# Kept left sums and more seven-product pairs in the closing products of a two-layer decoder trunk

## The chip, the cores and the metric

The kernel runs on one core of a Trainium2 chip, in one launch. The metric is device microseconds of one execution, as the median of several. The engines that matter are TensorE (PE, matrix products and transposes), VectorE (DVE, elementwise work), ScalarE (ACT, casts and copies) and SyncE (SP), whose queue issues the DMA transfers of the weights. Each engine works through its own instructions in order and waits where an input or a free buffer is missing.

## The reference

Two decoder layers over 256 rows of width 2048, all in float32. Layer 0 mixes tokens by retention (8 heads), layer 1 by latent attention (MLA); each is followed by a SwiGLU feed-forward block of width 5632. Every sub-layer is wrapped in two RMS norms.

```python
for i in range(DEPTH):                      # DEPTH = 2
    h = rms_norm(x, norm_mix_pre[i])
    h = retention(h, ...) if i % 2 == 0 else mla(h, ...)
    x = x + rms_norm(h, norm_mix_post[i])
    h = rms_norm(x, norm_ffn_pre[i])
    x = x + rms_norm(swiglu(h, ffn_w_gu[i], ffn_w_down[i]), norm_ffn_post[i])

def swiglu(x, w_gu, w_down):
    gate, up = jnp.split(x @ w_gu, [D_FF], axis=-1)
    return (jax.nn.silu(gate) * up) @ w_down
```

Three products close a sub-layer: the retention's output (4096 to 2048, `rto` in the kernel), the MLA's output (2048 to 2048, `mlo`), and the down product of each feed-forward block (5632 to 2048, `dn`).

## The kernel before

**Tiling.** The 256 rows are two row tiles of 128. A product runs over k-tiles of 128 (its inner dimension) and over column groups of 1024, in four banks of 128x512: `b00` and `b01` for row tile 0, `b10` and `b11` for row tile 1. A float32 value is split into two parts, `hi` (a cast, on ACT) and `lo` (the rest, a subtraction on DVE), and each product is three matmuls: hi by hi, hi by lo and lo by hi. A k-tile costs 12 matmuls of 128x512, a pair of k-tiles 24.

**Weights.** They stream through the core once. SP loads a tile of 128x1024 (512 KB) into one of four `raw` buffers; `split` makes `hi` and `lo` in rings of five buffers each (`weights`). In gate and up (`gu`), in the retention's q/k and v/g products, `tile_load` gives the last one or two k-tiles of a group other space for hi and lo, borrowed from tiles that aren't filled yet (`spare`).

**Sevens.** A pair of k-tiles by two row tiles by two column halves is a 2x2 block product, and some pairs are made with seven products in place of eight (Winograd's form): 21 matmuls. That needs sums of four blocks of the left side (`left_sums`, four 128x128 operations and a split on DVE), sums of the weights (`right_sums`: four 128x512 operations on DVE, L250 to L253, and two splits of 128x1024), and three extra banks `m` that are combined at the end: after the last seven of a product, `combine` (L340 to L345) forms the combinations on DVE, and `add` (L350) adds one to each of the four banks. The adds of row tile 0 stand in the plan behind the first k-tile pair after the last seven, the adds of row tile 1 one pair later.

**Closing products.** `closing` runs a product in two column halves, one after the other. `parted` splits the left side of the next pair and, if that pair is a seven, makes its left sums, for each half anew. The sevens are the pairs 2, 5, 8, 11, 14, 17 of 22 in both halves of the down products, and the pairs 2, 6, 10 of 16 in both of the retention output; the MLA output has none. In the second half the last four k-tiles are skewed: row tile 0 runs ahead and row tile 1 follows, so that the norm's statistics of row tile 0 start early, and the last two k-tiles of row tile 0 go bank by bank.

**Gate and up.** Eleven groups per layer (`gu0_0` to `gu0_10`, `gu1_0` and on), each with 16 k-tiles. From the second group on, the first eight k-tiles are four sevens in a form of its own (`first_sevens`): the weights' sums are called a, b, c and d, each with hi and lo. Behind each group ACT takes the silu of the gate half, DVE multiplies it by the up half into `fa` (L995), PE transposes `fa` in two batches of four (L962, banks `ftp`) and ACT copies the result (`aT`), the left side of the down product. `later(n, ...)` puts such work n loading steps into the next group.

**Order.** The program's order on each engine is set by the kernel's plan lists and then by a scheduler. Loads are issued in the order of use; a load waits for its `raw` buffer to be free.

Of the kernel before, what the change touches and what calls it, by code (L numbers as in the profile page):

```python
# [35 lines left out]
DN_SEVENS = (2, 5, 8, 11, 14, 17)  # L36
RTO_SEVENS = (2, 6, 10)
# [20 lines left out]
def trunk(  # L58
# [141 lines left out]

    def split(hi, lo, src, g=None):

        if g is None:
            nc.scalar.copy(out=hi, in_=src)  # L204
            nc.vector.tensor_sub(out=lo, in0=src, in1=hi.bitcast(F32))  # L205
# [6 lines left out]
    def weights(load, parts, name, room=None):  # L212

        raw = wp.tile([P, 1024], F32, tag="raw", bufs=RAW, name=f"{name}_raw")
# [4 lines left out]
        else:  # L219
            hi, lo = room(f"{name}_xhi"), room(f"{name}_xlo")  # L220
# [312 lines left out]
    def tile_load(w, g, name, halves=0, spare=(0, None)):  # L533
# [4 lines left out]
        def load(kt, first_half=False):  # L538
# [8 lines left out]
            return weights(dma, parts, f"{name}_w{kt}", spare[1] if kt >= DT - spare[0] else None)  # L547
# [6 lines left out]
    hT = hp.tile([P, DT, 2, NT, P], F32R, tag="hT", name="hT")  # L554
# [21 lines left out]
    def norm_piece(t, i, ssq, col):  # L576
# [13 lines left out]
        split(hT[:, ks, 0, t, :], hT[:, ks, 1, t, :], part)  # L590
# [31 lines left out]
    def closing(act, kts, w, g_post, col, name, gain_tile, skew=4, sevens=(), sums=None):  # L622
# [36 lines left out]

        parted(0, 0)  # L660
        for half in range(2):
# [45 lines left out]
            def first_done(banks):  # L707
# [11 lines left out]
                between=first_done if half else None, sevens=sevens,  # L719
                left=lambda p, half=half: parts["s", half, p],  # L720
# [16 lines left out]
    def retention():  # L737
# [43 lines left out]
        with tc.tile_pool(name="rt_s", bufs=1) as sp:  # L781
# [81 lines left out]
            with tc.tile_pool(name="rt_v", bufs=1) as rp:  # L863
# [3 lines left out]
                def spare_y(name):  # L867
                    return rp.tile([P, 1024], F32R, tag="yT", bufs=RH, name=name)
# [61 lines left out]
                def sums():  # L930
                    both = ("vh", "vl")[sums.n % 2]
                    sums.n += 1
                    s = rp.tile([P, 2, 4, P], F32R, tag=both, bufs=1, name="rs")
# [7 lines left out]
                    lambda name: rp.tile([P, 1024], F32, tag="sg", bufs=1, name=name), sevens=RTO_SEVENS, sums=sums,  # L941
# [3 lines left out]
    def swiglu(i):  # L945
        with tc.tile_pool(name=f"ff{i}", bufs=1) as fp:
# [4 lines left out]
            def spare_a(name):  # L951
                return fp.tile([P, 1024], F32R, tag="aT", bufs=groups, name=name)
# [14 lines left out]
            def sums(n=0):  # L967
# [12 lines left out]
            for j in range(groups):  # L980
                name = f"gu{i}_{j}"
                spare = min(2, (groups - j) // 2), spare_a
# [8 lines left out]
                for t in range(NT):  # L991
# [385 lines left out]
```

## Time and profile before

| what | value |
|---|---|
| time, median of 3 runs | 2427.02 us (2423.98 to 2428.43) |
| the profiled execution, its own time | 2426.71 us |
| its span, first to last instruction | 2424.9 us |
| mean granted TensorE clock | 0.998 |
| ACT busy | 1479.1 us (61%) |
| DMA | 463.75 MB, 191 GB/s |

The profile's page gives busy times of each engine; a window gives the same for a stretch of the span. A row of the timeline has the start, the duration, the engine, the line, and what is written from what; in brackets stand the idle time ahead of it and what ended that. Matmuls are pipelined: a 128x512 matmul shows some 0.39 us of duration, while the next starts earlier, so their cost is read from start to start. A row of the chain of waits has a start, a duration, an engine and line, and the number of instructions. In a row of groups stand, behind the first bar, the busy time and the mean ns of one, and behind the second the idle time ahead of the group and its releaser. The stages follow each other so (us from the start of the span): the retention up to about 560, its output to 733, gate and up of layer 0 to 1207, its down product to 1440 (first half up to 1324), MLA with its output up to about 1710, gate and up of layer 1 to 2184, its down product to the end.

### The profile page before, as it was taken

What the parts mean: (1) busy time and instruction counts of PE and PEld (TensorE: products, weight loads), DVE (VectorE), ACT (ScalarE), POOL (GpSimd) and SP (SyncE); (2) the same over time, 40 slices, a digit from 0 to 9 for tenths busy, and PEclk for the clock granted to TensorE, in tenths of its full rate; (3) what the DMA queues carried; (4) which work ended last, traced back from release to release, by engine and by line L of the source; (5) the groups of instructions that cost most, each with busy time, mean ns of one, the idle gap of its engine ahead of it and who ended that gap; (6) DMA issues with size and microseconds to landing.
All of it is one profiled execution on the core that took longest, in us unless ns stands there. A gap on an engine that the chain in (4) does not pass through costs nothing.

```text
span 2424.9 us, 30707 instructions
## 1 busy us (share of the span) xinstructions
PE 2403.3 (99%) x10888; PEld 1975.1 (81%) x10888; DVE 2122.0 (88%) x3034; ACT 1479.1 (61%) x2082; POOL 23.9 (1%) x38
## 2 busy tenths in 40 slices
PE   9999999999999999999999999999999999999998
PEld 7888888888888787888888888888877888888887
DVE  8878989887879999899989987876899999998997
ACT  6545666665656666666666665655666666666664
POOL 0000000000000000000000000000000000000000
PEclk9999999999999999999999999999999999999999
DMA  7565565556665565656456654446656565556655
GB/s 273 171 211 185 164 206 194 165 172 203 192 213 193 195 213 184 217 172 216 168 194 214 207 185 148 130 137 198 202 182 215 180 211 202 188 183 202 206 194 164
DMA packets 129610, 463.75 MB, mean 191 GB/s; under 512 B 14640, under 2 KB 15024, under 8 KB 129456
## 3 DMA queue, kind: packets, MB, share of 16 engines
q1 hardware_dynamic: 129456, 461.80, 57.7%
q8 instruction: 85, 1.39, 0.2%
q14 instruction: 69, 0.57, 0.1%
HBM read 459.64 MB, written 2.10 MB: 190 GB/s over the span
## 4 chain that ended last, share of the span: by engine, by line
PE 80%; DVE 12%; DMA 4%; issue 2%; ACT 2%; SPq 0%; POOL 0%; DVEq 0%; ACTq 0%; POOLq 0%
PE gu_b L409 23%; PE dn_b L409 16%; PE rvg_b L409 14%; PE rto_b L409 6%; PE rqk_b L409 5%; PE mlo_b L409 3%; PE q L409 3%; PE dn_m L409 3%; DMA gu_w_raw<-w_gu 2%; DVE gu_blo L205 2%; DVE gu_alo L205 1%; PE mc_b L409 1%; DVE gu_w_lo L205 1%; DVE gu_t L449 1%; DVE gu_clo L205 1%
## 5 line engine op out<-in xcount | busy, mean ns | idle before, releaser
L409 PE MATMUL gu_b<-gu_w_hi,hT 128*128 128x512 f32 x1248 | 342.0, 390 | 0.0
L409 PEld LDWEIGHTS gu_b<-gu_w_hi,hT 128*128 128x128 f32 x1248 | 233.1, 188 | 49.0 <-DVE hT L205 0.9
L204 ACT CAST dn_w_hi<-dn_w_raw 128x1024 fp32r<-128x1024 f32 (+1 forms) x176 | 172.8, 993 | 95.2 <-DMA dn_w_raw<-w_down 44.4
L205 DVE TENSOR_TENSOR gu_w_lo<-gu_w_raw,gu_w_hi 128x1024 fp32r<-128x1024 f32 x156 | 185.5, 1218 | 48.4 <-ACT gu_w_hi L204 48.3
L204 ACT CAST gu_w_hi<-gu_w_raw 128x1024 fp32r<-128x1024 f32 x156 | 158.1, 1048 | 92.9 <-DMA gu_w_raw<-w_gu 73.2
L205 DVE TENSOR_TENSOR dn_w_lo<-dn_w_raw,dn_w_hi 128x1024 fp32r<-128x1024 f32 (+1 forms) x176 | 196.1, 1146 | 9.2 <-ACT dn_w_hi L204 8.9
L409 PE MATMUL gu_b<-gu_w_lo,hT 128*128 128x512 f32 x624 | 193.3, 390 | 0.0
L409 PE MATMUL dn_b<-dn_w_hi,dn_ah 128*128 128x512 f32 x536 | 169.3, 390 | 0.0
L409 PE MATMUL dn_b<-dn_w_lo,dn_ah 128*128 128x512 f32 x536 | 169.0, 389 | 0.0
L409 PE MATMUL dn_b<-dn_w_hi,dn_al 128*128 128x512 f32 x536 | 168.9, 389 | 0.0
L409 PE MATMUL rvg_b<-rvg_w_hi,hT 128*128 128x512 f32 x552 | 149.8, 390 | 0.0
L409 PEld LDWEIGHTS gu_b<-gu_w_lo,hT 128*128 128x128 f32 x624 | 116.6, 188 | 25.3 <-DVE gu_w_lo L205 1.3
L409 PEld LDWEIGHTS rvg_b<-rvg_w_hi,hT 128*128 128x128 f32 x552 | 103.4, 188 | 21.4
L409 PEld LDWEIGHTS dn_b<-dn_w_hi,dn_al 128*128 128x128 f32 x536 | 100.6, 188 | 21.0
L409 PEld LDWEIGHTS dn_b<-dn_w_lo,dn_ah 128*128 128x128 f32 x536 | 100.6, 188 | 20.9
L409 PEld LDWEIGHTS dn_b<-dn_w_hi,dn_ah 128*128 128x128 f32 x536 | 100.3, 188 | 20.4
L409 PE MATMUL rqk_b<-rqk_w_hi,hT 128*128 128x512 f32 x384 | 106.0, 392 | 2.2 <-ACT rqk_w_hi L204 1.5
L204 ACT CAST gu_ahi<-gu_ta 128x1024 fp32r<-128x1024 f32 x80 | 84.3, 1054 | 35.1 <-DVE gu_ta L452 17.1
L205 DVE TENSOR_TENSOR rvg_w_lo<-rvg_w_raw,rvg_w_hi 128x1024 fp32r<-128x1024 f32 x69 | 82.3, 1222 | 25.5 <-ACT rvg_w_hi L204 25.1
L204 ACT CAST gu_bhi<-gu_t 128x512 fp32r<-128x512 f32 x80 | 49.7, 621 | 85.9 <-DVE gu_t L449 85.8
L204 ACT CAST rvg_w_hi<-rvg_w_raw 128x1024 fp32r<-128x1024 f32 x69 | 71.1, 1051 | 46.0 <-DMA rvg_w_raw<-ret_vg 34.7
L205 DVE TENSOR_TENSOR gu_alo<-gu_ta,gu_ahi 128x1024 fp32r<-128x1024 f32 x80 | 97.7, 1221 | 0.0
(487 smaller groups left out, 6109.5 us busy)
## 6 DMA issues: line engine op xcount, KB each, us to landing
gu_w_raw<-w_gu SPq DMA_DIRECT2D x192, 512.0 KB, 4.3
dn_w_raw<-w_down SPq DMA_DIRECT2D x176, 512.0 KB, 4.4
gu_s<-w_gu SPq DMA_DIRECT2D x160, 512.0 KB, 4.4
rvg_w_raw<-ret_vg SPq DMA_DIRECT2D x80, 512.0 KB, 4.4
rto_w_raw<-ret_out SPq DMA_DIRECT2D x64, 512.0 KB, 4.4
rqk_w_raw<-ret_qk SPq DMA_DIRECT2D x51, 512.0 KB, 4.5
rvg_s<-ret_vg SPq DMA_DIRECT2D x48, 512.0 KB, 4.3
mlo_w_raw<-mla_out SPq DMA_DIRECT2D x32, 512.0 KB, 3.6
```

Of the source, the lines that this page charges most:

```text
L204: nc.scalar.copy(out=hi, in_=src)
L205: nc.vector.tensor_sub(out=lo, in0=src, in1=hi.bitcast(F32))
L409: nc.tensor.matmul(out, e[2](), e[3](), start=bank not in begun, stop=ends[bank, added.get(bank, 0)] == n, skip_group_check=bank in added,)
L449: nc.vector.tensor_add(out=t2[p], in0=ta[:, 0:512], in1=b11)
```

## The change

It has four parts.

1. The left sums of a closing product are made once, when a pair first needs them, and kept for the second half. Their space is the former one tile `hT` (the normalised left side of the products before), which is now four tiles of four k-tiles each, in a ring of four with the sums; the name `hx(k)` replaces it in code.
2. The sevens differ by half: the down products have six in the first half as before and eight in the second (10 and 19 are new, 19 is the last); the retention output has four and five in place of three and three.
3. `share` divides the borrowed space in gate and up, q/k and v/g: next to hi and lo for the last one or two k-tiles, up to two raw tiles of the k-tiles ahead of the last two are put there.
4. The transposes of `fa` come two loading steps later.

```diff
-DN_SEVENS = (2, 5, 8, 11, 14, 17)
-RTO_SEVENS = (2, 6, 10)
+DN_SEVENS = (2, 5, 8, 11, 14, 17), (2, 5, 8, 10, 11, 14, 17, 19)
+RTO_SEVENS = (3, 6, 9, 12), (3, 5, 6, 9, 12)
...
+    def share(slots, room):
+
+        both = 2 if slots >= 6 else 1 if slots >= 3 else 0
+        return min(2, slots - 2 * both), both, room
...
-        raw = wp.tile([P, 1024], F32, tag="raw", bufs=RAW, name=f"{name}_raw")
+        if raw_room is None:
+            raw = wp.tile([P, 1024], F32, tag="raw", bufs=RAW, name=f"{name}_raw")
+        else:
+            raw = raw_room(F32, f"{name}_xraw")
...
-            return weights(dma, parts, f"{name}_w{kt}", spare[1] if kt >= DT - spare[0] else None)
+            raws, both, room = spare
+            return weights(
+                dma, parts, f"{name}_w{kt}", room if DT - 2 - raws <= kt < DT - 2 else None,
+                room if kt >= DT - both else None,
+            )
...
-    hT = hp.tile([P, DT, 2, NT, P], F32R, tag="hT", name="hT")
+
+    hT = {}
+
+    def hx(k):
+        if k // 4 not in hT:
+            hT[k // 4] = hp.tile([P, 4, 2, NT, P], F32R, tag="h8", bufs=4, name="hT")
+        return hT[k // 4]
...
-            if b in sevens:
-                f, hi, lo = sums()
+            if b in sevens[half] and b not in sums:
+                if len(sums) % 2 == 0:
+                    room[0] = hp.tile([P, 2, 2, 4, P], F32R, tag="h8", bufs=4, name=f"{name}_s")
+                f = wp.tile([P, 4, P], F32, tag="mv", bufs=MV, name=f"{name}_sf")
+                hi, lo = (room[0][:, len(sums) % 2, i] for i in range(2))
                 left_sums(a[:, 0, 0], a[:, 1, 0], a[:, 0, 1], a[:, 1, 1], f, hi, lo)
-                parts["s", half, b] = hi, lo
+                sums[b] = hi, lo
...
+        hT.clear()
         parted(0, 0)
...
-                between=first_done if half else None, sevens=sevens,
-                left=lambda p, half=half: parts["s", half, p],
+                between=first_done if half else None, sevens=sevens[half],
+                left=lambda p: sums[p],
...
-                        banks = vg_group(h, (min(2, (RH - h) // 2), spare_y))
+                        banks = vg_group(h, share(RH - h, spare_y))
...
-                spare = min(2, (groups - j) // 2), spare_a
+                spare = share(groups - j, spare_a)
...
-                    later(2 + t, lambda j=j, t=t, a=a: transposes(j, t, a))
+                    later(4 + t, lambda j=j, t=t, a=a: transposes(j, t, a))
```

The left out lines pass `hx(k)` where `hT` stood, give the new arguments on, and remove the two functions that made space for left sums in `rto` and `dn`. In the program the 128x512 matmuls go from 9854 to 9833. On DVE the 128x512 operations go from 1359 to 1385, the 128x128 ones from 196 to 160, the 128x1024 ones from 861 to 868. The transfers on SP are 899 before and after.

**DVE, second half of layer 0's down product, behind pair 8** (`w8_ta` and `w8_tb` are sums of pair 8's weights, that is of k-tiles 16 and 17; `w18` is a k-tile). Before:

```order
L205 TENSOR_TENSOR dn01_w8_talo_12123<-dn01_w8_ta_12116,dn01_w8_tahi_12122 128x1024
L205 TENSOR_TENSOR dn01_w8_tblo_12127<-dn01_w8_tb_12117,dn01_w8_tbhi_12126 128x1024
L205 TENSOR_TENSOR dn0_al_12152<-aT05_8859,dn0_ah_12151 128x512
L205 TENSOR_TENSOR dn01_w18_lo_12158<-dn01_w18_raw_12155,dn01_w18_hi_12157 128x1024
L205 TENSOR_TENSOR dn01_w19_lo_12176<-dn01_w19_raw_12173,dn01_w19_hi_12175 128x1024
L205 TENSOR_TENSOR dn01_w20_lo_12207<-dn01_w20_raw_12204,dn01_w20_hi_12206 128x1024
L205 TENSOR_TENSOR dn01_w21_lo_12225<-dn01_w21_raw_12222,dn01_w21_hi_12224 128x1024
```

And of the change, at the same place:

```order
L210 TENSOR_TENSOR dn01_w8_talo_12117<-dn01_w8_ta_12110,dn01_w8_tahi_12116 128x1024
L259 TENSOR_TENSOR dn01_w10_ta_12209<-dn01_w20_raw_12197 128x512
L260 TENSOR_TENSOR dn01_w10_ta_12209<-dn01_w20_raw_12197,dn01_w21_raw_12203 128x512
L210 TENSOR_TENSOR dn01_w8_tblo_12121<-dn01_w8_tb_12111,dn01_w8_tbhi_12120 128x1024
L261 TENSOR_TENSOR dn01_w10_tb_12210<-dn01_w10_ta_12209,dn01_w21_raw_12203 128x512
L210 TENSOR_TENSOR dn0_al_12146<-aT05_8920,dn0_ah_12145 128x512
L210 TENSOR_TENSOR dn01_w18_lo_12160<-dn01_w18_raw_12155,dn01_w18_hi_12157 128x1024
L210 TENSOR_TENSOR dn01_w19_lo_12178<-dn01_w19_raw_12175,dn01_w19_hi_12177 128x1024
L210 TENSOR_TENSOR dn01_w20_lo_12200<-dn01_w20_raw_12197,dn01_w20_hi_12199 128x512
L262 TENSOR_TENSOR dn01_w10_tb_12210<-dn01_w10_tb_12210,dn01_w21_raw_12203 128x512
L210 TENSOR_TENSOR dn01_w21_lo_12206<-dn01_w21_raw_12203,dn01_w21_hi_12205 128x1024
```

Two sums of pair 10 (of k-tiles 20 and 21) now stand ahead of the last split of pair 8.

**The end of the same product, DVE** (`mv` and `mx` are the combinations, `b00` to `b11` the banks). Before, where the last seven is pair 17:

```order
L205 TENSOR_TENSOR dn01_w38_lo_12629<-dn01_w38_raw_12626,dn01_w38_hi_12628 128x1024
L343 TENSOR_TENSOR dn01_mv1_12572<-dn01_m5_11846,dn01_mv1_12572 128x512
L345 TENSOR_TENSOR dn01_mx_12578<-dn01_m5_11846,dn01_mv2_12573 128x512
L205 TENSOR_TENSOR dn0_al_12623<-aT010_10719,dn0_ah_12622 128x512
L350 TENSOR_TENSOR dn01_b00_11721<-dn01_b00_11721,dn01_mv0_12571 128x512
L350 TENSOR_TENSOR dn01_b01_11722<-dn01_b01_11722,dn01_mv1_12572 128x512
```

Of the change, where it is pair 19:

```order
L210 TENSOR_TENSOR dn01_w42_lo_12697<-dn01_w42_raw_12694,dn01_w42_hi_12696 128x1024
L352 TENSOR_TENSOR dn01_mv1_12656<-dn01_m5_11858,dn01_mv1_12656 128x512
L354 TENSOR_TENSOR dn01_mx_12662<-dn01_m5_11858,dn01_mv2_12657 128x512
L210 TENSOR_TENSOR dn01_w43_lo_12703<-dn01_w43_raw_12700,dn01_w43_hi_12702 128x1024
L359 TENSOR_TENSOR dn01_b00_11742<-dn01_b00_11742,dn01_mv0_12655 128x512
L359 TENSOR_TENSOR dn01_b01_11743<-dn01_b01_11743,dn01_mv1_12656 128x512
```

A 1024-wide split of the last k-tile takes the place of a 512-wide one ahead of the adds. On PE, before, the twelve matmuls of row tile 1 for k-tiles 36 and 37 stand between the last matmul of row tile 0 that the adds wait for and the next one into `b00`; of the change, nothing does:

```order
L418 MATMUL dn01_b00_11742<-dn01_w41_lo_12683,dn0_ah_12604 128x512
L418 MATMUL dn01_b01_11743<-dn01_w41_lo_12683,dn0_ah_12604 128x512
L418 MATMUL dn01_b00_11742<-dn01_w41_hi_12682,dn0_al_12605 128x512
L418 MATMUL dn01_b01_11743<-dn01_w41_hi_12682,dn0_al_12605 128x512
L418 MATMUL dn01_b00_11742<-dn01_w42_hi_12696,dn0_ah_12664 128x512
L418 MATMUL dn01_b00_11742<-dn01_w42_lo_12697,dn0_ah_12664 128x512
```

The add into `b00` (L359 above) belongs between the third and the fifth of these rows.

**Gate and up of layer 0, group 4, PE** (`ftp030` and `ftp031` are the transposes of group 3's `fa`; `bhi`, `ahi` and so on are this group's weight sums). Before, the transposes stand behind nine matmuls of the group:

```order
L409 MATMUL gu0_4_b10_8093<-gu0_4_ahi_8103,sl0_6616 128x512
L962 MATMUL ftp030_8124<-cst_73,fa_8084 128x128 x4
L962 MATMUL ftp031_8132<-cst_73,fa_8084 128x128 x4
L409 MATMUL gu0_4_b00_8091<-gu0_4_bhi_8142,hT_90 128x512
L409 MATMUL gu0_4_b00_8091<-gu0_4_blo_8143,hT_90 128x512
```

Of the change they stand behind 21:

```order
L418 MATMUL gu0_4_b11_8124<-gu0_4_ahi_8133,sl0_6644 128x512
L980 MATMUL ftp030_8185<-cst_73,fa_8114 128x128 x4
L980 MATMUL ftp031_8193<-cst_73,fa_8114 128x128 x4
L418 MATMUL gu0_4_b00_8121<-gu0_4_bhi_8203,hT_6607 128x512
L418 MATMUL gu0_4_b00_8121<-gu0_4_blo_8204,hT_6607 128x512
```

The product `fa` itself (L995, now L1013) stands five 128x512 operations later among DVE's rows of the group. Further on in groups 2 to 4, the product with `dhi` stood ahead of the run of `chi` into `b01`; of the change it stands behind it. In group 10 it is the other way round.

More of the change, by code (lines that the diff above doesn't have):

```diff
@@ L210, in split, with weights @@
             )
-    def weights(load, parts, name, room=None):
-        raw = wp.tile([P, 1024], F32, tag="raw", bufs=RAW, name=f"{name}_raw")
+    def weights(load, parts, name, raw_room=None, room=None):
+        if raw_room is None:
+            raw = wp.tile([P, 1024], F32, tag="raw", bufs=RAW, name=f"{name}_raw")
+        else:
+            raw = raw_room(F32, f"{name}_xraw")
         load(raw)
@@ L219, in weights @@
         else:
-            hi, lo = room(f"{name}_xhi"), room(f"{name}_xlo")
+            hi, lo = room(F32R, f"{name}_xhi"), room(F32R, f"{name}_xlo")
         for a, n, g in parts:
@@ L531, in first_sevens, with tile_load @@
         return banks
-    def tile_load(w, g, name, halves=0, spare=(0, None)):
+    def tile_load(w, g, name, halves=0, spare=(0, 0, None)):
         def load(kt, first_half=False):
@@ L589, in norm_piece @@
         )
-        split(hT[:, ks, 0, t, :], hT[:, ks, 1, t, :], part)
+        split(hx(k0)[:, ks, 0, t, :], hx(k0)[:, ks, 1, t, :], part)
         if watch[0] is not None:
@@ L619, in next_input, with closing @@
         return piece
-    def closing(act, kts, w, g_post, col, name, gain_tile, skew=4, sevens=(), sums=None):
+    def closing(act, kts, w, g_post, col, name, gain_tile, skew=4, sevens=((), ())):
         last = col is None
@@ L629, in closing @@
         r = {}
-        parts = {}
+        parts, sums, room = {}, {}, [None]
         def parted(half, b):
@@ L847, in retention @@
                 rope_s = rp.tile([P, NT, NF_R], F32, name="rope_s")
-                spare = 1, lambda name: rp.tile([P, 1024], F32R, tag="spare", bufs=2, name=name)
+                spare = share(3, lambda kind, name: rp.tile([P, 1024], kind, tag="spare", bufs=3, name=name))
                 for gq in range(4):
@@ L865, in retention, with spare_y @@
                 yT = {}
-                def spare_y(name):
-                    return rp.tile([P, 1024], F32R, tag="yT", bufs=RH, name=name)
+                def spare_y(kind, name):
+                    return rp.tile([P, 1024], kind, tag="yT", bufs=RH, name=name)
                 def take_y(k0, n):
@@ L940, in retention @@
                     take_y, RH * 4, ret_out, g_mix_post[0], G_FFN, "rto",
-                    lambda name: rp.tile([P, 1024], F32, tag="sg", bufs=1, name=name), sevens=RTO_SEVENS, sums=sums,
+                    lambda name: rp.tile([P, 1024], F32, tag="sg", bufs=1, name=name), sevens=RTO_SEVENS,
                 )
@@ L949, in swiglu, with spare_a @@
             aT = {}
-            def spare_a(name):
-                return fp.tile([P, 1024], F32R, tag="aT", bufs=groups, name=name)
+            def spare_a(kind, name):
+                return fp.tile([P, 1024], kind, tag="aT", bufs=groups, name=name)
             def take_a(k0, n):
@@ L965, in transposes, with sums @@
                 )
-            def sums(n=0):
+            def sums(n):
                 f = wp.tile([P, 4, P], F32, tag="mv", bufs=MV, name=f"sf{i}")
@@ L1001, in swiglu @@
                 None if i else G_MIX + DT, f"dn{i}",
-                lambda name: fp.tile([P, 1024], F32, tag="fa", bufs=1, name=name), sevens=DN_SEVENS, sums=sums,
+                lambda name: fp.tile([P, 1024], F32, tag="fa", bufs=1, name=name), sevens=DN_SEVENS,
             )
```

13 lines of the change are left out of this document (3 added, 10 removed).

## The prediction

> **What bounds the kernel now.** I read the page's busy times first, then the chain that ended last, then the windows of the stages, then single rows where TensorE (PE) waits.
>
> ```profile
> span 2424.9 us, 30707 instructions
> ...
> PE 2403.3 (99%) x10888; PEld 1975.1 (81%) x10888; DVE 2122.0 (88%) x3034; ACT 1479.1 (61%) x2082; POOL 23.9 (1%) x38
> ...
> 1300.45 34.68 PE dn_b L409 x153
> ...
> 775.00:1207.00 432.00, 428.26 (x1905) 348.94 (x1904) 402.24 (x528) 272.13 (x347) 0.00 (x0) 1.00 0.59 193
> ...
> 1324.00:1440.00 116.00, 116.00 (x516) 96.08 (x515) 103.57 (x143) 70.42 (x94) 0.55 (x1) 1.00 0.61 199
> ```
>
> PE is busy 99% of the span, so time goes only by fewer matmuls or by shorter waits of PE. The chain's piece at 1300.45 gives the price of a 128x512 matmul: 34.68/153 = 0.2267 us apart (their single durations overlap). In layer 0's down product, second column half (1324 to 1440), PE is busy 116.00 of 116.00 us and VectorE (DVE) 103.57: nothing is lost there now, and DVE has some 11% to spare. In layer 0's gate and up (775 to 1207) PE is idle 3.7 us of 432, though DVE is at 93%. Each place needs its own answer.
>
> **Part 1, fewer matmuls.** A pair of k-tiles made as a "seven" has 21 matmuls, an ordinary one 24. The down products go from 12 to 14 sevens in each layer, the retention output from 6 to 9: 2x2+3 = 7 more, 21 matmuls less. 21 x 0.2267 = **-4.76 us**, if PE stays fed.
>
> **Part 2, what DVE does for it.** These are its rows around the seven of pair 8 in the first half of layer 0's down product, with PE's:
>
> ```profile
> 1236.36 4.63 DVE L205 TENSOR_TENSOR dn_w_lo<-dn_w_raw,dn_w_hi 128x1024 fp32r<-128x1024 f32 x4 [0.26 <-ACT dn_w_hi L204]
> 1240.91 0.69 DVE L205 TENSOR_TENSOR dn_al<-aT,dn_ah 128x512 fp32r<-128x512 f32 x1
> 1241.51 0.69 DVE L250 TENSOR_TENSOR dn_w_ta<-dn_w_raw 128x512 f32<-128x512 f32 x1
> ...
> 1245.64 0.68 DVE L253 TENSOR_TENSOR dn_w_tb<-dn_w_tb,dn_w_raw 128x512 f32<-128x512 f32 x1
> 1246.24 0.69 DVE L205 TENSOR_TENSOR dn_al<-aT,dn_ah 128x512 fp32r<-128x512 f32 x1
> ...
> 1249.26 1.23 DVE L205 TENSOR_TENSOR dn_w_tblo<-dn_w_tb,dn_w_tbhi 128x1024 fp32r<-128x1024 f32 x1 [0.59 <-ACT dn_w_tbhi L204]
> ...
> 1250.65 0.39 PE L409 MATMUL dn_m<-dn_w_hi,dn_ah 128*128 128x512 f32 x1
> ...
> 1254.05 0.39 PE L409 MATMUL dn_m<-dn_w_tbhi,sh 128*128 128x512 f32 x1
> ...
> dn_w_raw<-w_down SPq DMA_DIRECT2D x176, 512.0 KB, 4.4
> ```
>
> Start to start a 512-wide operation takes 0.60 us (1240.91 to 1241.51), a 1024-wide one 1.14 (4.55/4). A seven costs DVE six of the first and three of the second, 7.0 us, for 21 x 0.2267 = 4.76 of PE; an ordinary pair 2.9 for 5.44. So a seven is a debt of 2.3 and an ordinary pair repays 2.6. Sevens two or three pairs apart repay; the second half's 10 and 11, adjacent behind 8, don't. Against that the left sums are made once: 30 become 21, 36 operations of 128x128 fewer, all on a DVE that has room there, so by themselves they bring PE nothing.
>
> In pair 8 the last sum is ready at 1250.5, and PE takes it at 1254.05: a lead of 3.5 us. In the changed order DVE makes the first two sums of pair 10 ahead of that last split, and one of them needs k-tile 21, whose buffer comes free with the sum at 1245.64 (done at 1246.24), 4.4 us of PE time before pair 8 starts. With 4.4 us to land and 0.3 to be asked for it is there 0.3 us after pair 8's start; one sum of 0.6 and one split of 1.14 bring the last part of pair 8 to 2.1 us, where it is due at 3.4. Going on so through pairs 9, 10 and 11, k-tile 23's split ends at 15.6 (due 15.9), pair 11's last at 17.8 (due 18.6). Leads of 0.3 to 0.8, but leads. The same reckoning for 17 to 19 leaves 0.5, for the retention output's 5 and 6 0.1. I take **+0.5 us** for all; ends 0 and +3.
>
> **Part 3, the end of the down product.** The final seven moves from pair 17 to pair 19. Before, the row behind it stands like this:
>
> ```profile
> 1413.17 0.39 PE L409 MATMUL dn_m<-dn_w_hi,dn_ah 128*128 128x512 f32 x1
> ...
> 1420.65 0.61 PE L409 MATMUL dn_b<-dn_w_hi,dn_ah 128*128 128x512 f32 x2
> ...
> 1423.37 0.61 PE L409 MATMUL dn_b<-dn_w_hi,dn_ah 128*128 128x512 f32 x2
> ...
> 1420.32 0.68 DVE L205 TENSOR_TENSOR dn_al<-aT,dn_ah 128x512 fp32r<-128x512 f32 x1
> 1420.92 1.29 DVE L350 TENSOR_TENSOR dn_b<-dn_b,dn_mv 128x512 f32<-128x512 f32 x2
> ```
>
> DVE adds the seven's combinations to the banks (L350) from 7.75 us behind the seven's start, and PE accumulates on them at 1423.37, because 12 matmuls of the other row tile (1420.65 to 1423.37, 2.72 us) stand between. With pair 19 they don't: the two last k-tiles go bank by bank, so PE goes from k-tile 41 straight to bank 00 of k-tile 42, at 33 x 0.2267 = 7.48 us behind the seven's start. DVE's queue ahead of the add has a 1024-wide split where a 512-wide one stood, 0.53 more: the add starts at 8.28 and ends some 0.7 later, at 9.0. PE waits about 1.5 to 1.6 us, in both layers: **+3.2 us** (ends +2, where only the hand-over itself of some 0.9 each is left, the add and its signals, and +7, where DVE comes a further 0.4 late and the clock falls as below). Behind the waiting matmul stands all that is left of the product, and behind that the statistics of its rows, so nothing covers this wait. The retention output has its run of the other row tile still in between: 0.
>
> **Part 4, gate and up.** The rows:
>
> ```profile
> 867.34 0.74 DVE L995 SCALAR_TENSOR_TENSOR fa<-gu_b,rto_x_r,fsg 128x512 f32<-128x512 f32 x1
> 868.00 0.68 DVE L205 TENSOR_TENSOR gu_blo<-gu_t,gu_bhi 128x512 fp32r<-128x512 f32 x1
> 868.60 0.74 DVE L995 SCALAR_TENSOR_TENSOR fa<-gu_b,rto_x_r,fsg 128x512 f32<-128x512 f32 x1
> ...
> 868.36 0.60 PE L962 MATMUL ftp<-cst,fa 128*128 128x128 f32 x4
> 869.39 0.66 PE L962 MATMUL ftp<-cst,fa 128*128 128x128 f32 x4 [0.44 <-DVE fa L995]
> ...
> L962 PE MATMUL ftp<-cst,fa 128*128 128x128 f32 x176 | 25.7, 277 | 2.0 <-DVE fa L995 1.5
> ...
> L409 PE MATMUL gu_b<-gu_dhi,hT 128*128 128x512 f32 x160 | 54.3, 396 | 2.3 <-ACT gu_mv L479 2.3
> ...
> 881.77 0.50 PE L409 MATMUL gu_b<-gu_dhi,hT 128*128 128x512 f32 x1 [0.32 <-ACT gu_mv L479]
> ...
> ACT gu_w_hi L204 <- DMA gu_w_raw<-w_gu: 73.2, 45, 3.4
> DVE gu_w_lo L205 <- ACT gu_w_hi L204: 48.3, 46, 2.0
> ACT dn_w_hi L204 <- DMA dn_w_raw<-w_down: 44.4, 42, 2.2
> ```
>
> Four transposes take 0.44, so the second four were due at 868.80 and began at 869.39: 0.59 lost, where the row prints 0.44 of idle. The same reckoning over the 20 groups of both layers gives 12 such losses, 3.9 us together (the group row's 2.0, and some 0.16 for each refill). Now the transposes stand 12 matmuls later (2.72 us), and the product `fa` stands five 512-wide operations (3.0 us) later in DVE's queue. That alone would be a draw. But ACT waits 73 us for raw gate/up tiles and DVE 48 us for ACT's casts: two more raw tiles let the tail of a group load earlier, and I reckon that DVE gets to the next group's sums up to 2.7 us earlier, so `fa` would be ready some 1.3 us ahead of need. The queue that issues the transfers (SP) carries the same 512 KB tiles in the same order; only the moment at which a buffer lets each go changes. Transposes and `fa` are followed on PE and DVE by sevens whose parts already wait in buffers, so what comes early there isn't lost again. I take -3.8.
>
> Second, the parts of the columns: in six groups (2 to 4 of each layer) the product with `gu_dhi`, the last to be combined, came ahead of the `gu_chi` run and waited for ACT's copy (0.32 idle, 0.49 by starts, then 0.3 for what follows). Now it goes last there. Groups that have that order already lose 0.3 in place of 0.85: 6 x 0.55 = -3.2. In group 10 of both layers the order goes the other way: 2 x 0.55 = +1.1. Sum **-5.9 us**; ends -8 (nearly all of both losses) and +1.3 (below).
>
> **Part 5, the rest.** The smaller shares in the retention's stages and the new order at the boundary to layer 1's first product: 0, ends -2 and +2, since PE idles there less than 10 us in all.
>
> Sum: -4.76 +0.5 +3.2 -5.9 = -7.0 against the profiled run's 2426.71 (span 2424.9 and 1.8 around it): 2419.7. That run lies 0.3 below the median of the three: **2420.0 us**.
>
> **The clock.** One row shows what a gap may bring:
>
> ```profile
> 1458.15 1.17 PE L409 MATMUL mc_b<-mc_w_hi,hT 128*128 128x512 f32 x2 [1.99 <-ACT hT L204]
> ...
> 1458.00:1462.00 4.00, 3.85 (x10) 3.04 (x11) 3.09 (x4) 2.32 (x9) 0.00 (x0) 0.57 0.55 197
> ```
>
> After 1.99 us of idle the granted clock was 0.57 over the next 4 us, and the matmuls stood 0.43 apart, some 1.5 us lost. [...] Whether 1.55 is enough no row shows; I take 0, with +1.5 in each layer as rival C.
>
> **The rivals.**
> - A. *Gate and up don't gain* (the change doesn't do what it says there). For it: DVE is 93% busy, and if the ring of five hi and lo tiles, not the raw tiles, holds the stream back, `fa` comes 3.0 later against 2.72: 0.3 x 12 = +3.4 where I have -3.8. Then -4.76 +0.5 +3.2 +3.4 -2.1 = +0.2: 2427; with half of it, **2424 to 2427**. Against it: ACT's wait is put down to the DMA.
> - B. *Slower: the adjacent sevens run dry.* Each cluster has two k-tiles that DVE must have before older work goes on. If they land later than about 5.0 us (4.4 and the lead of 0.3 to 0.5), PE stops. Waits of up to 2.2 us for such tiles occur (the longest of `dn_w_raw` in the waits above); at 1.9 in each of five clusters (two in each down product, one in the retention output), +9.5, and with gate and up at -2: -4.8+9.5+3.2-2 = +5.9, **2433**. Against it: the median landing of 4.4.
> - C. *The clock halves behind the gap of part 3*: +3, **2423**.
> - D. *No gap of note* (the add hands over in 0.9 each) and all of gate and up: -4.76+0+1.8-8 = -11, **2416**; with part 5 at -2, 2414.
>
> **How the numbers follow.** Forecast 0.50, A 0.20, B 0.08, C 0.10, D 0.12. About 0.2%, 4.9 us, is what a measurement of this kernel can tell from no change: faster is below 2422.2, slower above 2431.9. Of the forecast (its own range 2417 to 2423) four fifths lie below 2422.2, of C a third, of D all, of A a tenth: 0.40+0.03+0.12+0.02 = 0.57. Slower is B: 0.07. The range reaches over A and D with their bounds and leaves out B: 2412 to 2429.
>
> **What will show it.** Matmuls of 128x512 in gate/up, down and retention output: 21 fewer. Part 2: no idle before `dn_m` or `dn_b` rows in pairs 8 to 12 and 17 to 19 of the second halves. Part 3: one wait of 1.3 to 1.8 us for the add's line ahead of a `dn_b` row, some 7.5 us behind the last seven of each layer; clock 1.00 behind it. Part 4: idle before `ftp` below 0.5 us in all, before `gu_dhi` about 1. I am wrong if PE waits in the second halves for sums, if `ftp` waits grow, or if the add finds DVE free early.

## The result and the profile after

The changed kernel takes 2408.22 us in the median of 4 runs (2406.36 to 2410.52), against 2427.72 before (2423.98 to 2429.53): a ratio of 0.9922, 95% interval 0.9905 to 0.9939. The forecast was faster, at 2420.0 and not under 2412; 7 us of gain were expected, and 19.5 came. The profiled execution took 2408.83 us. Its page begins so (span; busy time and share of each engine; the chain's shares):

```profile
span 2407.1 us, 30750 instructions
...
PE 2389.2 (99%) x10867; PEld 1974.4 (82%) x10867; DVE 2137.3 (89%) x3031; ACT 1480.0 (61%) x2087; POOL 31.2 (1%) x38
...
PE 88%; DVE 7%; DMA 2%; ACT 1%; issue 1%; POOL 0%; SPq 0%; DVEq 0%; POOLq 0%; ACTq 0%
```

PE has 21 matmuls less, as the order showed, and is busy 14.1 us less (2403.3 to 2389.2); the span is 17.8 shorter. The chain that ended last ran through PE for 80% before and 88% now, through DVE for 12% and now 7%, through DMA for 4% and now 2%: PE waits for the others less. Where, the chain's pieces show (start, length, engine and line, number of instructions):

```profile
869.73 40.84 PE gu_b L418 x180
911.44 40.88 PE gu_b L418 x180
953.20 40.84 PE gu_b L418 x180
...
1290.90 34.68 PE dn_b L418 x153
```

A whole group of gate and up, 180 matmuls, is one piece of 40.84 us: 0.227 each, the spacing of the down product (34.68/153). Before, no piece of gate and up was longer than 38.95.

For the rest I read the loss by starts: the distance from each matmul to the next, less the usual distance of its size (0.2268 us for 128x512, 0.109 for a transpose of 128x128), summed over a stage. In us:

| stage | before | after | part of the forecast |
|---|---|---|---|
| gate and up, both layers | 19.4 | 5.1 | 4: -5.9 |
| down products, both layers | 0.0 | 4.5 | 2 and 3: +3.7 |
| retention output | 0.2 | 0.1 | 2 |
| boundary to the MLA and its first product | 5.5 | 2.1 | 5: 0 |
| retention's v/g | 3.6 | 2.5 | 5: 0 |
| start and q/k | 6.7 | 7.9 | 5: 0 |
| the rest of the MLA | 3.5 | 3.4 | - |
| sum | 38.9 | 25.6 | |

The 13.3 us less of loss and the 21 matmuls (4.8) make 18.1; the span is 17.8 shorter. The greatest part, 14.3 us, is gate and up. The window of layer 0's gate and up, as shown of before (the stretch, its length, then busy time and count of PE, PEld, DVE, ACT and POOL, the granted clock, the DMA share and GB/s):

```profile
770.00:1198.00 428.00, 427.54 (x1923) 353.53 (x1922) 407.64 (x537) 274.22 (x353) 0.00 (x0) 1.00 0.59 197
```

The groups of the `dhi` products and of the transposes (busy time, mean ns of one, idle time ahead):

```profile
L418 PE MATMUL gu_b<-gu_dhi,hT 128*128 128x512 f32 x160 | 52.7, 390 | 0.0
...
L980 PE MATMUL ftp<-cst,fa 128*128 128x128 f32 x176 | 22.8, 272 | 0.0
```

And the view of waits (total, times, longest):

```profile
ACT gu_w_hi L209 <- DMA gu_w_raw<-w_gu: 12.7, 10, 2.7
...
DVE gu_w_lo L210 <- ACT gu_w_hi L209: 8.7, 13, 1.7
```

PE's idle time in the window falls from 3.7 us to 0.5, the idle time ahead of `ftp` from 2.0 to 0.0 and ahead of `dhi` from 2.3 to 0.0. What changed upstream is in the waits: ACT's for raw tiles 73.2 to 12.7 us, DVE's for ACT's casts 48.3 to 8.7. The lead itself is in the timeline's rows of DVE and PE at the start of group 3, where the late `fa` (the product of group 2) was shown of before:

```profile
849.32 0.69 DVE L457 TENSOR_TENSOR gu_ta<-gu_s 128x512 f32<-128x512 f32 x1
...
863.80 0.75 DVE L1013 SCALAR_TENSOR_TENSOR fa<-gu_b,rto_x_r,fsg 128x512 f32<-128x512 f32 x1
...
865.06 0.75 DVE L1013 SCALAR_TENSOR_TENSOR fa<-gu_b,rto_x_r,fsg 128x512 f32<-128x512 f32 x1
...
868.70 1.03 PE L980 MATMUL ftp<-cst,fa 128*128 128x128 f32 x8
```

The second `fa` ends at 865.81 and is taken at 869.13, in the second half of the eight transposes: 3.3 us early, where it came 0.6 late before. DVE starts the group's sums at 849.32, 14.6 us ahead of PE's first matmul of the group (863.93); before, the two stood at 856.47 and 866.31, 9.8 us apart. The gain of lead is 4.8 us.

The other side, the end of layer 0's down product (timeline of DVE and PE):

```profile
1420.47 1.22 DVE L210 TENSOR_TENSOR dn_w_lo<-dn_w_raw,dn_w_hi 128x1024 fp32r<-128x1024 f32 x1
1421.61 1.89 DVE L359 TENSOR_TENSOR dn_b<-dn_b,dn_mv 128x512 f32<-128x512 f32 x3
...
1422.45 0.47 PE L418 MATMUL dn_b<-dn_w_hi,dn_ah 128*128 128x512 f32 x1 [1.47 <-DVE dn_b L359]
```

And two windows around it:

```profile
1418.00:1422.00 4.00, 2.98 (x14) 2.12 (x12) 4.00 (x6) 1.72 (x2) 0.00 (x0) 1.00 0.82 231
1422.00:1426.00 4.00, 3.55 (x16) 2.94 (x17) 3.94 (x8) 1.13 (x3) 0.00 (x0) 1.00 0.67 216
```

PE stands 1.47 us for the add, 1.63 by starts, and again 1.63 in layer 1. The split of 1024 is ahead of the add, as in the order. The granted clock is 1.00 ahead of the gap and behind it.

### The profile page after: what moved, and what is told of

The parts are those of the page before. It is cut to its first block, busy times and chain, and to the rows that moved or that the text cites. A ratio compares the mean times of both kernels' runs of the same rounds, so it can differ in the third digit from the quotient of the medians.

```text
span 2407.1 us, 30750 instructions
## 1 busy us (share of the span) xinstructions
PE 2389.2 (99%) x10867; PEld 1974.4 (82%) x10867; DVE 2137.3 (89%) x3031; ACT 1480.0 (61%) x2087; POOL 31.2 (1%) x38
## 4 chain that ended last, share of the span: by engine, by line
PE 88%; DVE 7%; DMA 2%; ACT 1%; issue 1%; POOL 0%; SPq 0%; DVEq 0%; POOLq 0%; ACTq 0%
PE gu_b L418 32%; PE dn_b L418 15%; PE rvg_b L418 14%; PE rto_b L418 6%; PE rqk_b L418 5%; PE mlo_b L418 3%; PE q L418 3%; PE dn_m L418 3%; PE mc_b L418 1%; PE rto_m L418 1%; DVE gu_w_lo L210 1%; PE ftp L980 1%; PE ry L908 1%; DMA gu_w_raw<-w_gu 1%; DMA gu_s<-w_gu 0%
## 5 line engine op out<-in xcount | busy, mean ns | idle before, releaser
L418 PE MATMUL gu_b<-gu_w_hi,hT 128*128 128x512 f32 x1296 | 353.5, 390 | 0.0
L418 PEld LDWEIGHTS gu_b<-gu_w_hi,hT 128*128 128x128 f32 x1296 | 242.1, 188 | 50.9 <-DVE hT L210 0.9
L418 PE MATMUL dn_b<-dn_w_hi,dn_ah 128*128 128x512 f32 x508 | 160.9, 390 | 2.9 <-DVE dn_b L359 2.9
L418 PE MATMUL dn_b<-dn_w_lo,dn_ah 128*128 128x512 f32 x508 | 161.0, 390 | 0.3 <-DVE dn_w_lo L210 0.3
L418 PE MATMUL dn_b<-dn_w_hi,dn_al 128*128 128x512 f32 x508 | 160.6, 389 | 0.0
L210 DVE TENSOR_TENSOR gu_w_lo<-gu_w_raw,gu_w_hi 128x1024 fp32r<-128x1024 f32 x122 | 143.6, 1225 | 6.8 <-ACT gu_w_hi L209 6.7
L209 ACT CAST gu_w_hi<-gu_w_raw 128x1024 fp32r<-128x1024 f32 x122 | 122.4, 1050 | 29.1 <-DMA gu_w_raw<-w_gu 12.7
L210 DVE TENSOR_TENSOR gu_clo<-gu_s,gu_chi 128x1024 fp32r<-128x1024 f32 x80 | 97.4, 1221 | 14.4 <-ACT gu_chi L209 13.2
L209 ACT CAST gu_bhi<-gu_s 128x512 fp32r<-128x512 f32 x80 | 49.7, 622 | 78.9 <-PE gu_b L418 67.5
L209 ACT CAST gu_chi<-gu_s 128x1024 fp32r<-128x1024 f32 x80 | 83.8, 1051 | 13.6 <-PE gu_b L418 13.6
```

What stands on the lines that cost most here:

```text
L418: nc.tensor.matmul(out, e[2](), e[3](), start=bank not in begun, stop=ends[bank, added.get(bank, 0)] == n, skip_group_check=bank in added,)
```

## The experiments

The reason first held for the gain (theory R): with only four raw buffers the loads of a group's last k-tiles and of the next group's first came late, ACT's casts with them, and DVE had too little lead; the raw tiles in borrowed space give it. Rivals: the later transposes (L), and the kept sums with the split of `hT` (S). Edits are against the changed kernel unless another is named, and so are differences; all runs were timed beside the kernel before, which stood at 2427.5 to 2427.7. Each loss is read from one profiled execution: with the borrowed space and the transposes as before, gate and up lost 19.4, 21.6 and 22.1 us in three kernels, so differences of up to some 3 us in a stage aren't clear of that spread.

**The third and fourth part out.**

```diff
-        both = 2 if slots >= 6 else 1 if slots >= 3 else 0
-        return min(2, slots - 2 * both), both, room
+        return 0, min(2, slots // 2), room
...
-                    later(4 + t, lambda j=j, t=t, a=a: transposes(j, t, a))
+                    later(2 + t, lambda j=j, t=t, a=a: transposes(j, t, a))
```

> The change without its third and fourth parts: borrowed space holds hi and lo of the last one or two k-tiles only, as before, and the transposes of fa come two loading steps earlier, as before; the kept left sums and the new sevens stay. Theory R (the extra raw tiles freed the stream of gate and up): the loss of PE by starts in gate and up is back at some 19 us in both layers (5 in the changed kernel), so about 2423 us, and ACT waits some 70 us for gate/up tiles. Theory S (the kept sums and the split of hT freed gate and up): the loss stays near 5 us, about 2409.

Measured: 2426.37 us, ratio to before 0.9996 (0.9987 to 1.0006). Loss in gate and up 21.6 us, in the down products 5.8. So the closing products' part of the change, by itself, isn't to be told from no change, and S falls.

**Only the raw tiles out** (the first of the two edits; in groups 6, 7 and 9 it also puts back a borrowed pair of hi and lo that `share` had given up for raw tiles), and **only the transposes early** (the second):

> The change with no raw tile in the borrowed space (hi and lo of the last one or two k-tiles only, by the rule of before); late transposes and the closing products as changed. Theory R (raw tiles): loss in gate and up 14 to 22 us, 2418 to 2426. Theory L (the later transposes did it): loss 4 to 8 us, 2408 to 2411.

> The change with the transposes of fa two loading steps earlier, as before; raw tiles in the borrowed space and the closing products as changed. Theory R (raw tiles): the product fa is ready so early that little is lost, loss in gate and up 5 to 9 us, 2408 to 2412. Theory L (later transposes): loss 14 us or more, 2417 or more.

Measured: without raw tiles 2422.96 us, loss in gate and up 18.3; with early transposes 2410.82, loss 7.2. The waits of the kernel without raw tiles stand where they stood before the change:

```profile
ACT gu_w_hi L208 <- DMA gu_w_raw<-w_gu: 67.9, 44, 4.1
DVE gu_w_lo L209 <- ACT gu_w_hi L208: 48.6, 41, 2.7
```

R holds: the raw tiles are worth 13.2 us of loss (14.7 of time). The later transposes are worth 2.1 (2.6) beside them and some 3 of the 21.6 without them; the first is not clear of the noise, since the runs of the two kernels overlap (2409.64 to 2414.05 and 2406.36 to 2410.52).

**One raw tile in place of two.**

```diff
-        return min(2, slots - 2 * both), both, room
+        return min(1, slots - 2 * both), both, room
```

> The change with at most one extra raw tile in place of two in each group. If the stream is held back by the time from the freeing of a raw buffer to the landing of its next tile, each extra tile gives the same lead: the loss of gate and up by starts lies midway, 9 to 14 us (5 with two, 18 to 21 with none). If the first tile does nearly all of it: under 8 us.

Measured (one timed run): 2409.18 us, loss in gate and up 7.3. The first tile does nearly all: 11.0 us less of loss (18.3 to 7.3), where the second brings 2.2 (7.3 to 5.1). A wait of PE is what is left when the lead is used up; once the lead is long enough, more of it is worth little.

**A fifth raw buffer, paid for with a hi and lo buffer**, in the kernel before:

```diff
-    RAW, WB, MV = 4, 5, 6
+    RAW, WB, MV = 5, 4, 6
```

> The kernel before with five raw buffers in place of four, paid for with one of the five hi and lo buffers. Theory R in its plain form (the raw ring holds gate and up back): the loss there falls from 19 us to under 12. Rival (the hi and lo ring is the limit as soon as it is shorter): the loss rises above 19, and the waits of ACT for the release of hi buffers by PE grow.

Measured: 2442.87 us, ratio 1.0067 (1.0053 to 1.0080). Loss in gate and up 24.3 us, in v/g 9.9 (3.6 before), in the down products 4.7 (0 before). ACT's waits:

```profile
ACT gu_bhi L204 <- DVE gu_t L449: 65.4, 34, 3.0
ACT dn_ah L204 <- PE dn_b L409: 65.2, 51, 1.6
ACT gu_w_hi L204 <- PE gu_b L409: 61.3, 70, 2.0
```

The wait of the casts `gu_w_hi` for the DMA is no longer in the list, and in its place ACT waits 61.3 us for PE to release hi buffers. So here a fifth raw buffer isn't worth the fifth hi and lo buffer. The rival was right, and R in its plain form ("the raw ring") says too little: the change leaves both rings as they are and takes the room for its raw tiles outside them. Part of that room wasn't in use before, but not all: in groups 6, 7 and 9 the raw tiles stand where a borrowed pair of hi and lo stood, and the groups behind them (7, 8 and 10), which lost 0.4 to 1.4 us before, lose at most 0.3.

**The kept sums alone.** The two edits of the first experiment, and the sevens of before (`DN_SEVENS` 2, 5, 8, 11, 14, 17 and `RTO_SEVENS` 2, 6, 10, in both halves).

> The first part of the change alone: left sums kept for the second half and hT split into four tiles; sevens, borrowed space and transposes as before. No matmul less, and DVE has room where the sums are saved: nothing in the down products; 2424 to 2428. The boundary to the MLA loses 5.5 us before and 2.1 in the changed kernel; if the split of hT is the reason, it falls to some 3.7 here, as it stood with the old sevens; if not, 5.5.

Measured: 2427.37 us, ratio 1.0000 (0.9991 to 1.0009); loss in the down products 0, at the boundary 5.7. Nine left sums less bring nothing, and the split of `hT` isn't the reason at the boundary.

**The old sevens, the rest as changed.**

> The change with the sevens of before (2, 5, 8, 11, 14, 17 in both halves of the down products; 2, 6, 10 in the retention output): 21 matmuls more, 4.8 us; no wait behind the last seven of a down product, 1.6 us less in each layer, and the one of 0.5 in layer 1 gone too. If those are all, 2408 to 2410, the same as the changed kernel, and the loss in the down products is back at 0. If the new sevens had a further effect (on the boundary to the MLA), 2411 or more.

Measured: 2408.00 us (2407.58 to 2409.03). Loss in the down products 0, at the boundary 3.7. The 21 matmuls and the waits cancel, as expected, within a microsecond. More sevens as placed here are worth nothing; all the gain is in the other half of the change.

**Can the sevens be had without the waits?** Theory W: the wait of 1.63 us comes of the missing run of row tile 1. Three ways to bring it back: another last pair, one seven fewer, or a shorter skew.

```diff
-DN_SEVENS = (2, 5, 8, 11, 14, 17), (2, 5, 8, 10, 11, 14, 17, 19)
+DN_SEVENS = (2, 5, 8, 11, 14, 18), (2, 5, 8, 10, 11, 14, 16, 18)
```

> The change with other sevens in the down products: 2, 5, 8, 11, 14, 18 in the first half and 2, 5, 8, 10, 11, 14, 16, 18 in the second, as many as in the change, but the last is pair 18, behind which a run of row tile 1 (k-tiles 38 and 39, 12 matmuls, 2.7 us) stands between the matmuls that the adds wait for and the next use of the banks. Theory W (the wait of 1.63 us comes of the missing cover): it is gone in both layers, 2404 to 2406, and the loss in the two down products falls from 2.2 to under 0.6 each. Rival (DVE is behind at the end of the product and the adds come late wherever they stand): a wait of 0.5 us or more stays.

Second, `(2, 5, 8, 10, 11, 14, 17)` in the second half:

> The change with seven sevens in the second half of the down products (2, 5, 8, 10, 11, 14, 17), so that pair 17 is the last, as before: 6 matmuls more than the change, 1.4 us, and by theory W 3.3 us of waits less: 2406 to 2407. If the crowding behind pair 8 (10 and 11 adjacent) cost anything, it shows here alone; I expect none.

Third:

```diff
-    def closing(act, kts, w, g_post, col, name, gain_tile, skew=4, sevens=((), ())):
+    def closing(act, kts, w, g_post, col, name, gain_tile, skew=2, sevens=((), ())):
```

> The change with the skew at the end of a second half at 2 in place of 4 k-tiles, pair 19 still the last seven: the run of row tile 1 for k-tiles 40 and 41 then stands ahead of bank 00 of k-tile 42, and its matmuls cover the adds. Theory W: the waits of 1.63 us go, 3.3 us in all; against it the last rows of row tile 1 end closer behind those of row tile 0, which uncovers up to 2.7 us of the norm's work at the end of each of four products. 2404 to 2410, with no wait of a dn_b matmul for the add.

Measured: 2408.18, 2406.48 and 2411.95 us. The wait for the add is gone in all three, in both layers: W holds. But only the second gains in the median (1.7 us of the 1.9 expected), and its runs (2404.69 to 2408.57) overlap the changed kernel's. The 2.0 us that its down products still lose are mostly waits of 0.3 to 0.9 us for the splits of pairs 9 and 11: the adjacent sevens do cost something, where none was expected. The shorter skew uncovers the ends: the loss rises by 2.0 us in the retention output and by 1.7 in the MLA output, and the time behind the last matmul goes from 8.5 to 11.0. And with pair 18 last the down products lose 5.8 us, in other places (timeline of DVE and PE, layer 0's second half):

```profile
1386.54 1.22 DVE L210 TENSOR_TENSOR dn_w_tblo<-dn_w_tb,dn_w_tbhi 128x1024 fp32r<-128x1024 f32 x1
1389.67 0.69 DVE L260 TENSOR_TENSOR dn_w_ta<-dn_w_raw 128x512 f32<-128x512 f32 x1 [1.92 <-DMA dn_w_raw<-w_down]
...
1391.49 2.35 DVE L210 TENSOR_TENSOR dn_w_lo<-dn_w_raw,dn_w_hi 128x1024 fp32r<-128x1024 f32 x2
...
1392.76 0.73 PE L418 MATMUL dn_b<-dn_w_lo,dn_ah 128*128 128x512 f32 x2 [1.23 <-DVE dn_w_lo L210]
```

PE waits at 1392.76 for an ordinary k-tile's split, which stands in DVE's queue behind a sum of the next seven (L260), and that waited 1.92 us for its raw tile.

**Sevens spaced out.** Theory D at this point was that adjacent sevens overload DVE.

```diff
-DN_SEVENS = (2, 5, 8, 11, 14, 17), (2, 5, 8, 10, 11, 14, 17, 19)
+DN_SEVENS = (2, 6, 8, 11, 15, 17), (2, 4, 6, 8, 11, 13, 15, 17)
```

> The change with as many sevens in the down products, but spaced: 2, 6, 8, 11, 15, 17 in the first half and 2, 4, 6, 8, 11, 13, 15, 17 in the second, none adjacent, pair 17 the last. By theory W the waits of 1.63 us at the end go (3.3 us), and by theory D (two adjacent sevens put DVE behind, every other pair does not: 9.9 us of DVE work for 10.2 of PE) nothing new comes: 2403 to 2405, loss in the two down products under 0.5 us each. If every other pair also puts DVE behind, losses of 1 us or more in the second halves, 2406 to 2409.

The same with `RTO_SEVENS = (2, 6, 8, 12), (2, 4, 6, 8, 10, 12)`:

> As the spaced sevens of the down products, and in the retention output 2, 6, 8, 12 in the first half and 2, 4, 6, 8, 10, 12 in the second: one seven more there, three matmuls, 0.7 us less if DVE keeps up: 2402 to 2405. If DVE does not, the loss in the retention output (0.07 in the changed kernel) rises to 1 us or more and it is even.

Measured: 2408.16 and 2414.39 us. Theory D falls. With the spaced sevens the down products still lose 5.7 us together; with the denser retention output that product loses 4.8. Of the loss in the down products, here as with pair 18 last, 1.03 us in each layer is a wait for a split of the last seven's own sums. DVE's queue, in layer 0's second half:

```profile
1367.18 1.22 DVE L210 TENSOR_TENSOR dn_w_talo<-dn_w_ta,dn_w_tahi 128x1024 fp32r<-128x1024 f32 x1
1368.71 0.69 DVE L259 TENSOR_TENSOR dn_w_ta<-dn_w_raw 128x512 f32<-128x512 f32 x1 [0.31 <-DMA dn_w_raw<-w_down]
1371.54 0.69 DVE L260 TENSOR_TENSOR dn_w_ta<-dn_w_raw 128x512 f32<-128x512 f32 x1 [2.13 <-DMA dn_w_raw<-w_down]
1372.14 1.22 DVE L210 TENSOR_TENSOR dn_w_tblo<-dn_w_tb,dn_w_tbhi 128x1024 fp32r<-128x1024 f32 x1
```

The window of that half:

```profile
1314.00:1431.00 117.00, 114.81 (x505) 93.64 (x504) 104.98 (x135) 69.12 (x90) 0.55 (x1) 1.00 0.58 194
```

DVE is busy 105 of 117 us; it isn't full, it stands, with the older seven's last split queued behind a sum whose raw tile hasn't landed. Hence theory Q: a seven holds its two raw tiles longer than ordinary k-tiles, so the raw ring of four is what dense sevens run into.

**Six raw buffers in the down products**, the two further ones in the space of gate and up's left sums, which is free by then; with the spaced sevens, with the change's own, and with pair 17 last:

```diff
+                more=lambda kind, name: fp.tile([P, 1024], kind, tag="xr", bufs=2, name=name),
...
-                dma, parts, f"{name}_w{kt}", room if DT - 2 - raws <= kt < DT - 2 else None,
+                dma, parts, f"{name}_w{kt}", more if more and kt % 3 == 2 else room if DT - 2 - raws <= kt < DT - 2 else None,
...
-                    hi = fp.tile([P, 4, P], F32R, tag="sa", bufs=4, name=f"sh{i}")
-                    lo = fp.tile([P, 4, P], F32R, tag="sa", bufs=4, name=f"sl{i}")
+                    s = fp.tile([P, 2, 4, P], F32R, tag="xr", bufs=2, name=f"s{i}")
+                    hi, lo = s[:, 0], s[:, 1]
```

> The spaced sevens (2, 6, 8, 11, 15, 17 and 2, 4, 6, 8, 11, 13, 15, 17), and every third raw tile of a down product in one of two further buffers, the space of gate and up's left sums, which is free by then: six raw buffers in place of four. Theory Q (DVE's queue stands behind sums that wait for a raw tile, since a seven holds its two raw tiles longer): the losses in the down products (3.4 and 2.2 us) fall under 1 each, 2403 to 2405. Rival (DVE's own work, 105 of 117 us with the sevens dense, or the five hi and lo buffers): they stay above 1.5 each, 2407 to 2409.

> The change itself with six raw buffers in the down products in place of four, nothing else. The waits of 1.63 us behind pair 19 don't hang on raw tiles and stay; the 0.6 of each down product beside them goes by theory Q: 2407 to 2408. No difference by the rival.

> Seven sevens in the second half of the down products (2, 5, 8, 10, 11, 14, 17) with six raw buffers there. With four, it lost 0.9 and 1.1 us in them and was at 2406.5. By theory Q these go: 2404 to 2405. By the rival: 2406 to 2407.

| sevens | four raw buffers: time, loss in the down products | six: time, loss |
|---|---|---|
| spaced, 17 last | 2408.16, 5.7 | 2404.65, 0.8 |
| of the change, 19 last | 2408.22, 4.5 | 2408.65, 6.1 |
| 10 and 11 adjacent, 17 last | 2406.48, 2.0 | 2406.38, 1.5 |

With spaced sevens Q holds. The same rows there (`xraw` is a tile in the further space), and behind them the same window:

```profile
1367.22 1.22 DVE L210 TENSOR_TENSOR dn_w_talo<-dn_w_ta,dn_w_tahi 128x1024 fp32r<-128x1024 f32 x1
1368.47 0.69 DVE L259 TENSOR_TENSOR dn_w_ta<-dn_w_xraw 128x512 f32<-128x512 f32 x1
1369.08 0.68 DVE L260 TENSOR_TENSOR dn_w_ta<-dn_w_xraw,dn_w_raw 128x512 f32<-128x512 f32 x1
1369.68 1.22 DVE L210 TENSOR_TENSOR dn_w_tblo<-dn_w_tb,dn_w_tbhi 128x1024 fp32r<-128x1024 f32 x1
```

```profile
1314.00:1431.00 117.00, 116.80 (x518) 96.08 (x518) 107.56 (x140) 73.50 (x98) 0.55 (x1) 1.00 0.55 187
```

DVE does more work in the stretch (107.6) and PE waits 0.2 us: DVE's own capacity wasn't the limit. This version is the fastest seen: 2404.65 us (2402.78 to 2406.11), ratio to before 0.9905 (0.9890 to 0.9920), and its slowest run is below the changed kernel's fastest (2406.36). For the other two the further buffers bring nothing to be measured, and there Q's forecast failed. With the change's sevens the waits behind pair 19 stay (1.65), as expected, but in both kernels waits of 0.3 to 1.3 us come anew in the first halves (at 1277.72 and 2246.14 with the change's sevens). DVE's rows ahead of the first of them:

```profile
1271.59 0.69 DVE L259 TENSOR_TENSOR dn_w_ta<-dn_w_raw 128x512 f32<-128x512 f32 x1 [2.20 <-DMA dn_w_raw<-w_down]
...
1276.45 2.35 DVE L210 TENSOR_TENSOR dn_w_lo<-dn_w_raw,dn_w_hi 128x1024 fp32r<-128x1024 f32 x2
```

This is the first sum of pair 17. It waits 2.20 us for its raw tile (3.02 in layer 1) and stands ahead of the splits of k-tiles 30 and 31, the first of which PE then waits for. In the changed kernel itself that sum stands behind those splits. So the queue stands here as it did with spaced sevens and four buffers: the further raw buffers helped only where the order on DVE didn't put a sum whose tile was still on its way ahead of a split that was due.

## Why the prediction was wrong

**Part 1** (21 matmuls, -4.76): right, in number and spacing.

**Part 2** (adjacent sevens, +0.5, ends 0 and +3): right in mechanism, and in place. I named k-tile 23's split as the closest, with 0.3 us of lead. The one wait over 0.15 us in the clusters is there, in layer 1's second half, pair 11:

```profile
2339.93 0.39 PE L418 MATMUL dn_b<-dn_w_hi,dn_ah 128*128 128x512 f32 x1
2340.65 0.50 PE L418 MATMUL dn_b<-dn_w_lo,dn_ah 128*128 128x512 f32 x1 [0.33 <-DVE dn_w_lo L210]
```

All in all the down products lose 1.2 us beside the adds (4.5 less 2 x 1.63). The reckoning that sevens two pairs apart repay counted DVE's work alone: with four raw buffers such sevens lost 5.7 us. Rival B, sums behind raw tiles that haven't landed, wasn't the case here at its price of 9.5, but its mechanism is real: with the spaced sevens six raw buffers took 4.9 of the 5.7 us away. The same rows stand in the version with pair 18 last, which wasn't run with six.

**Part 3** (the add's wait, 1.5 to 1.6 us in each layer): right; 1.63 in both, at the row and for the reason named.

**Part 4** (gate and up, -5.9, ends -8 and +1.3): the step that failed, in its size. It measured -14.3. Direction and agent were right: the raw tiles give DVE lead, `fa` comes early, and of rival A nothing is seen. By starts, the loss ahead of the transposes fell by 4.9 us (3.8 forecast), ahead of the `dhi` products by 3.9 (2.1 forecast, with what follows them), and ahead of all other rows by 5.5 (0 forecast). Two things were too small. The lead was put at "up to 2.7 us"; it is 4.8 in the group shown. And the losses that a lead can remove were put at the two kinds that have a name in the groups (3.9 for `ftp`, 0.55 for each of six `dhi` products), while the others were left to stand as they were. They went with it: `dhi` in full, not 0.55 of 0.85; `dlo` (0.44 twice), `chi` into `b01` (0.2 to 0.4 in 11 groups), and the 0.1 us steps behind each. The raw tiles took them away together; that DVE's small lead is the one cause between is read from the rows of one group. The end of -8 was called "nearly all of both losses", but the loss by starts of the whole stage was 19.4 us, which the trace of before held: behind the first group a group took 41.9 to 43.5 us, where 180 matmuls and 8 transposes need 41.7. That whole loss should have been the lower end.

**Part 5** (0, ends -2 and +2): short on one side. The v/g stage lost 1.1 us less, by the same raw tiles (3.3 to 3.6 in the kernels with none and the rings as before, 2.5 to 2.7 with them). The boundary to the MLA lost 3.4 less. Some 1.6 of that is the clock: granted at 0.50 from 1458.3 to 1461.6 before, with the matmuls 0.43 apart in place of 0.227, it stood at 1.00 over this boundary in the changed kernel (1440 to 1454). The rest goes with the last seven of the product ahead (2.1 to 2.3 us with pair 19 last and the skew of 4, raw tiles or not; 2.3 to 3.1 with pair 17 last and more sevens than before; 3.5 with pair 18 last; 3.7 with the old sevens and the raw tiles), and why it does is open. The start took 1.2 us more in this execution, in which the granted clock was 0.51 between 8 and 15 us, against 1.00 before; over the other kernels the start wanders between some 6 and 7.5, and no part of the change goes with it.

**Rivals C and D.** C didn't come: behind both waits of 1.63 us the granted clock was 1.00 (1422 to 1426, and 2386 to 2394 with the wait in it). D had the size of gate and up nearest, but not its reason: the gap it denied was there.

So the sum was short by 8.4 in part 4 and by 3.5 in part 5, and in parts 2 and 3 it lacked 0.8 of cost.

## What to carry to other kernels

Where one engine is behind in a stage and many rows of another wait a little for it, price a cure of the cause against the whole loss of that stage, read from starts against the issue rate, and not against the rows that show the wait by name. Look for staging space outside the rings before you trade one ring for another: two borrowed raw tiles gave 14 us here, a fifth raw buffer taken from the hi and lo ring cost 15. A saving where nothing waits for the engine (nine left sums, ratio 1.0000) is worth nothing, and a product with fewer matmuls is worth only what its operands' buffers and the order of the queue let it have: eight sevens in a half gave nothing with four raw buffers, nothing with six where they were adjacent and the last stood at pair 19, and 3.5 us with six, spaced, and pair 17 last.

## What the runs showed of the hardware

In these runs the granted clock doesn't follow the length of a single idle time. The first two fences are of the boundary to the MLA in the changed kernel with the old sevens (PE's timeline, and the window behind the gap), the next two of the boundary to gate and up of layer 0 in the kernel with the shorter skew:

```profile
1448.98 0.73 PE L418 MATMUL mc_b<-mc_w_hi,hT 128*128 128x512 f32 x2 [1.71 <-ACT hT L209]
```

```profile
1449.00:1453.00 4.00, 4.00 (x19) 3.28 (x20) 4.00 (x5) 3.46 (x11) 0.00 (x0) 1.00 0.67 248
```

```profile
731.00 0.83 PE L601 MATMUL htp<-cst,xs 128*128 128x128 f32 x4 [0.34 <-DVE xs L670]
...
733.21 0.97 PE L418 MATMUL gu_b<-gu_w_hi,hT 128*128 128x512 f32 x2 [1.13 <-ACT hT L209]
```

```profile
733.00:737.00 4.00, 3.79 (x10) 2.91 (x11) 2.98 (x7) 3.77 (x13) 0.99 (x1) 0.57 0.57 193
```

After one idle time of 1.71 us the granted clock was 1.00 over the stretch from 1449 to 1453. After two of 0.34 and 1.13 within 2.6 us it was 0.57 from 733 to 737, as it was over the four microseconds behind 1.99 before. So the clock was lower behind a shorter single idle time than behind a longer one. These rows don't show what decides, and no run was made to test it.
